# Two-layer decoder trunk on one core: rows of 2 KB for the first down weights of the two-chunk part, the reload of x behind the last streamed block, another order of the last sums, two lows by subtraction

## The chip, the cores and the metric

One core of a Trainium2 chip. The metric is device time in microseconds. The kernel before takes 1773.45 us, the median of three runs (1772.48 to 1774.38). Lower is better.

## The reference, cut to what matters

x is 1024 tokens of 1024 channels in float32. Two layers; in each a token mixer (layer 0 a causal convolution module, layer 1 a multi-scale pooling) and then a dense SwiGLU feed-forward of width 2816, each with RMS norm, shift, scale and gate from a conditioning vector, and a last RMS norm.

```python
def swiglu_ffn(h, w_gate, w_up, w_down):
    return (jax.nn.silu(h @ w_gate) * (h @ w_up)) @ w_down
...
        h = modulate(rms_norm(x, norm_ffn_g[i]), sh_f, sc_f)
        y = swiglu_ffn(h, ffn_w_gate[i], ffn_w_up[i], ffn_w_down[i])
        x = x + (1.0 + g_f)[:, None, :] * y
    return rms_norm(x, final_g)
```

The change touches only the feed-forward of layer 1.

## The kernel before

**Numbers and tiles.** Channels lie on the 128 partitions, tokens run along the free dimension. The tokens are cut into two chunks, A (the first 512) and B. Each float32 operand is split into a high part, `hi`, and the rest, `lo`, both of a rounded type that TensorE takes at full rate. A product is three matmuls, hi by hi, hi by lo and lo by hi, 128x128 weights against 128x512 activations. The width 2816 is 22 tiles `f`.

**Two ways to make a low part of a weight.** A weight arrives as `raw` by a DMA from SyncE's queue (SP) and ScalarE (ACT) copies it to `hi`. Then either VectorE (DVE) subtracts, `lo = raw - hi`, or ACT writes the rounded weight with its sign turned into `lo` and an accumulating DMA on GpSimd's queue (POOL) adds the weight from DRAM to it (`load_weight` with `summed`, L451 to L465, and `low_by_dma`, L1211). Units whose weights are marked `Own` (L608 to L631) take the subtraction.

**The feed-forward of layer 1** runs in three stages, all in the order in which `trunk` writes them at its end (L2164 to L2198):

1. Tiles f = 0 to 7 for chunk A alone (`ffn_p1`, `ffn_p2`).
2. *The two-chunk part*, `ffn_joint` (L1762): tiles f = 8 to 21 for both chunks, as 2x2 blocks with seven products in place of eight. A `joint_unit` (L1621) is one gate or one up matrix of a pair of tiles; it runs the blocks w11, w12, s2, s1, s3, s4 and w22, four steps k of three matmuls each (`block`, L1641). Some block operands don't fit on chip: `t1` and `t4` are kept in DRAM and read back for every unit (`streamed`, L1611, on the SP queue), `t4` for the last block, w22.
3. Tiles f = 0 to 7 for chunk B alone, the first two by `ffn_p1`, the others in pairs (`ffn_mixed`, L1362, with `final(A)`, the last norm of chunk A, beside them).

**The first end of the two-chunk part.** While the first joint unit runs, the down products of f = 6, 7 for chunk A are owed: eight outputs `d` of six matmuls, from four weight tiles of two outputs each (`JointDowns`, L1441, on `Downs`, L1224). Their lows come by an accumulating DMA each (`early`, L1247 to L1250); its source is two slices of `wdn`, so a row of it in DRAM is 1 KB and there are 256 rows. Behind them the block s2 begins. It needs `t2`, whose last piece DVE and ACT make at that time in `joint_rows` (L1564); they also make the last piece of `t4`, which is stored to DRAM and read back.

**The second end.** Within the two-chunk part x of chunk A lies in DRAM (`st["kept", "x"]`): the down products of each pair (`Seven`, L1486) are scaled into a tile `scaled` and added to it by accumulating DMAs on the POOL queue (L1547). In the last unit x comes back by eight DMAs of 256 KB on the POOL queue (L1753 to L1755). Each waits until its tile on chip is free and its row in DRAM is complete. Behind the last unit come the first tile of stage 3 (`before[:1]`, gate and up of f = 0 for chunk B), the down products of f = 20, 21 for both chunks (`last[:1]`, d = 0 to 3), the second tile (f = 1), and `last[1:]`, d = 4 to 7. The order of the sums is `JointDowns.todo`: for each d first A, then B.

PE's order is the order of the code. The orders of ACT, DVE, POOL and SP come out of a scheduler that the build runs. An instruction of a queue waits behind those ahead of it, and a DMA that has to wait holds up its queue.

Of the kernel before, what the change touches and what calls it, by code (L numbers as in the profile page):

```python
# [14 lines left out]
MUL, ADD, SUB = ALU.mult, ALU.add, ALU.subtract  # L15

P = 128
# [4 lines left out]
NF = F // P  # L22
# [37 lines left out]
WHOLE = 8  # L60
# [61 lines left out]


@with_exitstack
def trunk(ctx, tc, xT, c, vec, ada, adan, w1, w2, wgu, wdn, wpl, wph, out):
    nc = tc.nc
    ctx.enter_context(tc.manual_schedule(engines={mybir.EngineType.PE}))
    clock = {"PE": 0.0, "V": 0.0, "G": 0.0, "S": 0.0}
# [5 lines left out]
    last_mm, fixed = [None], [0.0025]  # L134
    synced = mybir.DependencyInfo(mybir.DependencyClass.Sync, mybir.DependencyReason.DATA)
    behind = [False]
# [7 lines left out]
    def order(ins):  # L144

        if behind[0] and last_mm[0] is not None:
            tc.add_manual_dep(ins.ins, last_mm[0], edge, reason="behind the products")
        return ins
# [378 lines left out]
    class Squares:  # L527
# [5 lines left out]
        def add(self, k):  # L533
            ch = self.ch
            if self.acc is None:
                self.acc = bank("acc") if self.psum else temp(ch.n, "acc", 2)
                S_.activation(self.acc, x[ch.i][k], AF.Square)
            else:
                sq = temp(ch.n)
                S_.activation(sq, x[ch.i][k], AF.Square)  # L540
                was = self.acc
                if self.psum and k == KT - 1:
                    self.acc = temp(ch.n, "acc", 2)
                V_.tensor_tensor(self.acc, was, sq, op=ADD)
# [69 lines left out]
    def own(unit_):  # L614
        return unit_[0], tuple(Own(w) for w in unit_[1])
# [608 lines left out]
    class Downs:  # L1224
# [13 lines left out]
        def load(self, dp):  # L1238
            if dp in self.tiles or dp not in self.dps:
                return  # L1240
            self.fetch()
            i = self.dps.index(dp)
            raw = self.raw[:, :, i * 2 * P : (i + 1) * 2 * P]
            wt = wts.tile([P, D], F32R, tag="w", name=nm("w")).rearrange("p (s f d) -> p s f d", s=2, f=2)
            with tc.high_priority(offset=-PREPARED):
                S_.copy(wt[:, 0], raw)
                if getattr(self, "early", False):  # L1247
                    S_.activation(wt[:, 1], raw, AF.Copy, scale=-1.0)
                    src = wdn[self.l, self.fs[0] : self.fs[0] + 2].rearrange("f p d -> p f d")[:, :, dp * 2 * P : (dp + 1) * 2 * P]
                    order(nc.gpsimd.dma_start(wt[:, 1], src, accum_op=ADD))  # L1250
                else:
                    V_.tensor_tensor(wt[:, 1], raw, f32(wt[:, 0]), op=SUB)
            self.tiles[dp] = wt
# [108 lines left out]
    def ffn_mixed(ch, l, plain, until, at_end=False, beside=None):  # L1362

        soon = plain == 2
        before = []
        for f in range(0, plain, 2):
            before += [ffn_p1(ch, l, f, True), ffn_p1(ch, l, f + 1, True, soon)]
            if f:
                before.insert(-1, own(ffn_p2(ch, l, [f - 2, f - 1], True)))
        mates = [Pair(ch, l, f, which) for f in range(plain, until, 2) for which in range(2)]  # L1370
        mine, theirs = [None] * len(mates), []
        for i, f in enumerate(range(plain - 2, until - 2, 2)):
            first, second = Downs(ch, l, (f, f + 1), (0, 1)), Downs(ch, l, (f, f + 1), (2, 3))
            for at, d in ((2 * i + 1, first), (2 * i + 2, second)):
                if at < len(mates):
                    mine[at] = d
                else:
                    theirs.append(d)
        last, = theirs
        before.insert(-1, (lambda take: mine[1].fetch(), ()))  # L1380
        paired = [(lambda take: mates[0].prepare(soon), ())]
        for i, me in enumerate(mates):
            if i + 1 == len(mates):
                paired.append((lambda take: reserve.__setitem__(0, 2), ()))
            paired.append(ffn_pair(ch, l, me, mates[i + 1] if i + 1 < len(mates) else None, mine[i], (mine + [last])[i + 1], soon and i == 0))
            if i == 1 and beside is not None:
                paired.append((lambda take: T.__setitem__(beside[0], Task(beside[1]())), ()))
        paired.append((lambda take: last.load(last.dps[1]), ()))
        if at_end:
            return before, paired, [alone(last), ending(ch, l, [until - 2, until - 1])]  # L1390
        rest = ffn(ch, l, True, at_end, until, ffn_p2(ch, l, [until - 2, until - 1], True))
        rest[1:1] = [alone(last)]
        rest[-3:-1] = rest[-2], rest[-3]
        for i in (4, -1):
            rest[i] = own(rest[i])
        return before, paired, rest
# [44 lines left out]
    class JointDowns(Downs):  # L1441


        def __init__(self, l, fs, dps, chs):
            super().__init__(None, l, fs, dps)
            self.todo = [(d, ch) for d in self.todo for ch in chs]

        def slot(self, out=None):
            d, ch = self.todo.pop(0)
# [171 lines left out]
    def joint_unit(l, me, following, downs, later, first=False, last=False):  # L1621

        def emit(take):
            wt = take()
# [9 lines left out]
            a, left, right = bank(name), bank(name), bank(name)  # L1634
# [3 lines left out]
            slots_at = () if first else SLOTS  # L1638
            at = [0]

            def block(out, part, acts, start):  # L1641
                for k, act in enumerate(acts):
                    cols = slice(k * P, (k + 1) * P)
                    for i, (wp, x_) in enumerate(((0, 0), (0, 1), (1, 0))):
                        matmul(out, w[part][wp][:, cols], act[x_], start=start and k + i == 0, stop=k == half - 1 and i == 2,
                               skip_group_check=True)
                    at[0] += 1
                    if at[0] in slots_at and downs:
                        for each in downs:
                            if each.todo:  # L1650
                                each.slot()
                                break
# [78 lines left out]
            if last:  # L1731
                for k, t in enumerate(front):
                    hi, lo = front[k] = slot(A, "hhi"), slot(A, "hlo")
                    S_.copy(hi, t)
                    V_.tensor_tensor(lo, t, f32(hi), op=SUB)
            block(a, "w22", t4, False)
            if last:
                st["h", 1] = front + hb[half:]
            else:
# [10 lines left out]
            if up and last:  # L1750
                for key, at_ in (("g11", (0, 0)), ("g21", (0, 1)), ("g12", (1, 0)), ("g22", (1, 1))):
                    st["g", at_[0], me.f + at_[1]] = st["blocks"][key]
                x[0] = x_first()  # L1753
                for t, src in zip(x[0], st["kept", "x"]):
                    nc.gpsimd.dma_start(t, src)  # L1755
            elif up:
                V_.scalar_tensor_tensor(qa, qb, -1.0, qa, op0=MUL, op1=SUB)
                given("t4", qa)
# [3 lines left out]
    def ffn_joint(l, start):  # L1762

        mates = [Joint(l, f, which) for f in range(start, NF, 2) for which in range(2)]
        whole = lambda f, chs: [JointDowns(l, (f, f + 1), dps, chs) for dps in ((0, 1), (2, 3))]
        mine = [whole(start - 2, (A,)), []]
        for f in range(start, NF - 2, 2):
            mine += [[Seven(l, (f, f + 1), half)] for half in range(2)]
        mine += [[each] for each in whole(NF - 2, (A, B))]

        mates[0].early = True
        for each in mine[0]:
            each.early = True

        def begin(take):
            mates[0].front()
            for each in mine[0]:
                for dp in each.dps:
                    each.load(dp)
        us = [(begin, ())]  # L1780
        for i, me in enumerate(mates):
            later = mine[i + 1]
            us.append(joint_unit(l, me, mates[i + 1] if i + 1 < len(mates) else None, mine[i], later[0] if later else None,
                                 i == 0, i + 1 == len(mates)))
        (second,), (final,) = mine[-2:]
        return us, [alone(second, final), alone(final)]
# [64 lines left out]
    def final(ch):  # L1851
        acc = yield from sum_sq(x[ch.i], ch.n, wide("acc"))
        rstd = yield from mean_rsqrt(acc, ch.n, True)
        for k in range(KT):
            xs = x[ch.i][k]
            V_.scalar_tensor_tensor(xs, xs, V("final_g", k), rstd, op0=MUL, op1=MUL)
            nc.sync.dma_start(out[:, k, ch.t0 : ch.t0 + ch.n], xs)
            yield
# [66 lines left out]
    for k in range(KT + 1):  # L1925
# [13 lines left out]
        if k < KT:  # L1939
# [6 lines left out]
            t = temp(A.n)  # L1946
# [243 lines left out]
    joint, last = ffn_joint(1, WHOLE)  # L2190
    add(joint)
    before, pairs, rest = ffn_mixed(B, 1, 2, WHOLE, True, ("final_a", lambda: final(A)))
    add(before[:1])
    put_eager(("T", 1), lambda: combined(B, (A, A, B, B)))

    add(last[:1] + before[1:] + last[1:])
    paired(B, pairs)
    add(rest)  # L2198
# [54 lines left out]
```

## Time and profile before

The profiled execution took 1771.89 us; its span, first to last instruction, is 1770.1 us.

| | busy us | share of the span |
|---|---|---|
| PE (matmul) | 1738.5 | 98% |
| DVE | 1374.0 | 78% |
| ACT | 987.1 | 56% |
| POOL | 564.0 | 32% |
| DMA, mean of 16 engines | | 207 GB/s over the span |

Times below count from the start of the span. The chain that ended last is 89% PE, so an idle stretch of PE is time of the kernel. The two-chunk part runs from about 1180 to 1602 us. A row of the timeline gives start, duration, engine, line, what is written and read, how often, and in brackets the idle time before it with what ended it. A row of windows gives the stretch, its length, PE's busy time with its matmuls, the granted clock (1.00 is full), the DMA engines' share and the rate.

### The profile page before, as it was taken

The page shows a single profiled execution, that of the slowest core. Times are in us where ns is not written, and L with a number is a line of the kernel's source. Part 1 is how long each engine was busy: PE and PEld are TensorE (multiplying, and loading weights), DVE is VectorE, ACT ScalarE, POOL GpSimd, SP SyncE. Part 2 cuts the span into 40 slices and gives each one's busy share as a digit, 9 for nine tenths or more (in the row PEclk, how much of TensorE's full clock was granted, in tenths as well). Part 3 has the DMA queues.
Part 4 walks back from the last instruction along what each step waited for, and adds up shares of the span by engine and source line. Part 5 has one row for each costly group of instructions (what it writes and reads, how often), then busy time and mean ns, then how long its engine had stood idle before and what let it go on. Part 6 is the DMA issues. An engine that isn't in the chain of part 4 may idle for free.

```text
span 1770.1 us, 24916 instructions
## 1 busy us (share of the span) xinstructions
PE 1738.5 (98%) x8830; PEld 1460.3 (82%) x8830; DVE 1374.0 (78%) x2273; ACT 987.1 (56%) x1566; POOL 564.0 (32%) x607
## 2 busy tenths in 40 slices
PE   9999999999999999999999999999999999999997
PEld 7777787788888888899999888887888888877996
DVE  7999657788775327989996977976888788777885
ACT  4776656767656455555555356464444444444653
POOL 0599614887834121211102713411011111111112
PEclk9999999999999999999999999999999999999999
DMA  9959746988988988877675477798778888887551
GB/s 296 305 171 251 196 118 157 243 214 213 240 204 205 240 218 195 222 210 215 198 213 132 123 179 177 166 235 272 226 216 262 240 242 223 252 251 201 155 150 54
DMA packets 145151, 366.26 MB, mean 207 GB/s; under 512 B 14977, under 2 KB 32641, under 8 KB 145026
## 3 DMA queue, kind: packets, MB, share of 16 engines
q1 hardware_dynamic: 109600, 265.56, 44.5%
q0 software_dynamic: 34272, 98.06, 31.3%
q8 instruction: 69, 1.13, 0.3%
q10 hardware_dynamic: 1154, 1.05, 0.2%
q14 instruction: 56, 0.46, 0.1%
HBM read 340.50 MB, written 24.12 MB: 206 GB/s over the span
## 4 chain that ended last, share of the span: by engine, by line
PE 89%; DMA 4%; issue 2%; DVE 2%; ACT 1%; POOL 1%; SPq 0%; DVEq 0%; POOLq 0%; ACTq 0%
PE gate L142 24%; PE dn L142 24%; PE up L142 23%; PE y L142 6%; PE a L142 3%; PE g L142 3%; PE first L142 2%; DMA adaw<-in_adan_dram 1%; DMA t<-t 1%; DMA w<-in_wdn_dram 1%; PE ada L142 1%; DMA front<-front 1%; DVE x L119 1%; ACT w L119 0%; DMA w<-in_wgu_dram 0%
## 5 line engine op out<-in xcount | busy, mean ns | idle before, releaser
L119 ACT CAST w<-raw 128x1024 fp32r<-128x1024 f32 (+1 forms) x314 | 262.7, 838 | 110.6 <-PE up L142 46.1
L142 PE MATMUL dn<-ghi,w 128*128 128x512 f32 (+1 forms) x944 | 302.6, 386 | 2.7 <-DMA w<-in_wdn_dram 2.1
L142 PE MATMUL gate<-hhi,w 128*128 128x512 f32 (+1 forms) x968 | 295.1, 373 | 1.3 <-ACT hhi L119 0.8
L142 PE MATMUL up<-hhi,w 128*128 128x512 f32 (+1 forms) x968 | 294.6, 372 | 0.0
L119 ACT ACTIVATE w<-raw 128x1024 fp32r<-128x1024 f32 (+1 forms) x182 | 172.9, 950 | 193.1 <-PE up L142 60.0
L119 DVE SCALAR_TENSOR_TENSOR x<-dn,gains,x 128x512 f32<-128x512 f32 (+1 forms) x312 | 225.5, 733 | 46.9 <-PE dn L142 45.2
L142 PEld LDWEIGHTS gate<-hhi,w 128*128 128x128 f32 x968 | 178.1, 189 | 34.6 <-ACT hhi L119 1.0
L142 PEld LDWEIGHTS dn<-ghi,w 128*128 128x128 f32 x944 | 176.3, 189 | 36.6 <-DMA w<-in_wdn_dram 2.5
L142 PEld LDWEIGHTS up<-hhi,w 128*128 128x128 f32 x968 | 178.0, 188 | 31.8
L142 PE MATMUL dn<-glo,w 128*128 128x512 f32 (+1 forms) x472 | 181.9, 385 | 0.1
L142 PE MATMUL gate<-hlo,w 128*128 128x512 f32 (+1 forms) x484 | 180.2, 372 | 0.3 <-DVE hlo L119 0.3
L142 PE MATMUL up<-hlo,w 128*128 128x512 f32 (+1 forms) x484 | 179.8, 372 | 0.0
L119 DVE SCALAR_TENSOR_TENSOR ca<-u,taps,ca 128x512 f32<-128x512 f32 x251 | 174.9, 747 | 0.9
L461 POOL DMA_DIRECT2D w<-in_wgu_dram x76 | 69.0, 907 | 247.3 <-ACT w L119 233.2
L1547 POOL DMA_DIRECT2D x<-scaled x48 | 41.6, 868 | 325.9 <-ACT scaled L119 170.2
L119 DVE TENSOR_TENSOR w<-raw,w 128x512 fp32r<-128x512 f32 (+1 forms) x132 | 108.9, 831 | 41.8 <-ACT w L119 34.9
L119 POOL TENSOR_TENSOR pa<-pa,pr 128x512 f32<-128x512 f32 x92 | 131.5, 1509 | 8.4 <-ACT pr L119 6.4
L119 DVE TENSOR_TENSOR t<-t,up 128x512 f32<-128x512 f32 (+1 forms) x76 | 49.4, 650 | 89.7 <-PE up L142 87.1
L1215 POOL DMA_DIRECT2D w<-in_wgu_dram x42 | 37.1, 891 | 256.3 <-ACT w L119 109.5
L119 POOL TENSOR_TENSOR pa<-pa,ny 128x512 f32<-128x512 f32 x77 | 104.0, 1381 | 8.5 <-ACT ny L119 5.8
L142 PEld LDWEIGHTS gate<-hlo,w 128*128 128x128 f32 x484 | 91.3, 189 | 16.6 <-DVE hlo L119 0.6
L142 PEld LDWEIGHTS up<-hlo,w 128*128 128x128 f32 x484 | 91.1, 188 | 15.9
(292 smaller groups left out, 3844.4 us busy)
## 6 DMA issues: line engine op xcount, KB each, us to landing
raw<-in_wgu_dram SPq DMA_DIRECT2D x148, 512.0 KB, 5.6
t<-t SPq DMA_DIRECT2D x224, 256.0 KB, 5.2
w<-in_wgu_dram POOLq DMA_DIRECT2D x76, 512.0 KB, 8.2
adaw<-in_ada_dram SPq DMA_DIRECT2D x64, 512.0 KB, 5.1
raw<-in_wdn_dram SPq DMA_DIRECT2D x62, 512.0 KB, 5.5
raw<-in_w_dram SPq DMA_DIRECT2D x42, 512.0 KB, 6.2
w<-in_wdn_dram POOLq DMA_DIRECT2D x34, 512.0 KB, 8.3
adaw<-in_adan_dram SPq DMA_DIRECT2D x32, 512.0 KB, 5.7
```

The lines of the kernel that those rows point to most:

```text
L119: self.last = self.order(getattr(self.eng, name)(out, *args, **kw))
L142: last_mm[0] = nc.tensor.matmul(out, lhsT, rhs, start=start, stop=stop, **kw).ins.name
L461: order(nc.gpsimd.dma_start(as_src(lo), src, accum_op=ADD))
L1215: order(nc.gpsimd.dma_start(lo, src, accum_op=ADD))
L1547: order(nc.gpsimd.dma_start(st["kept", "x"][at], t, accum_op=ADD))
```

## The change

Four edits. (1) The sources of the four early low DMAs come from a new DRAM array `wdp`, made on the host, in which the 512 numbers that a partition takes lie side by side: 128 rows of 2 KB for 256 of 1 KB. The hi parts and raw loads stay. (2) The eight reloads of x wait, by a semaphore, for the matmul that stood last on PE when step k = 3 of the last block w22 was written: the end of its step k = 2. (3) The last down sums run chunk by chunk, B first and then A. (4) Gate and up of f = 0 for chunk B (`before[0]`) are `Own`: DVE subtracts the two lows, in place of an ACT pass and an accumulating DMA of 512 KB each.

```diff
@@ Downs.load
                 if getattr(self, "early", False):
                     S_.activation(wt[:, 1], raw, AF.Copy, scale=-1.0)
-                    src = wdn[self.l, self.fs[0] : self.fs[0] + 2].rearrange("f p d -> p f d")[:, :, dp * 2 * P : (dp + 1) * 2 * P]
-                    order(nc.gpsimd.dma_start(wt[:, 1], src, accum_op=ADD))
+                    order(nc.gpsimd.dma_start(wt[:, 1].rearrange("p f d -> p (f d)"), wdp[dp], accum_op=ADD))
@@ JointDowns.__init__
-            self.todo = [(d, ch) for d in self.todo for ch in chs]
+            self.todo = [(d, ch) for ch in chs for d in self.todo]
@@ joint_unit
-            def block(out, part, acts, start):
+            def block(out, part, acts, start, came=None):
                 for k, act in enumerate(acts):
                     cols = slice(k * P, (k + 1) * P)
+                    if came is not None:
+                        came.append(last_mm[0])
...
-            block(a, "w22", t4, False)
+            came = []
+            block(a, "w22", t4, False, came)
...
                 for t, src in zip(x[0], st["kept", "x"]):
-                    nc.gpsimd.dma_start(t, src)
+                    d = nc.gpsimd.dma_start(t, src)
+                    tc.add_manual_dep(d.ins, came[3], synced, reason="behind the streamed block")
@@ ffn_joint
-        mine += [[each] for each in whole(NF - 2, (A, B))]
+        mine += [[each] for each in whole(NF - 2, (B, A))]
@@ trunk
     before, pairs, rest = ffn_mixed(B, 1, 2, WHOLE, True, ("final_a", lambda: final(A)))
+    before[0] = own(before[0])
     add(before[:1])
@@ kernel
+        "wdp": A(np.asarray(ffn_w_down)[1, (WHOLE - 2) * P : WHOLE * P].reshape(2, P, 4, 2 * P).transpose(2, 1, 0, 3).reshape(4, P, 4 * P)),
```

The POOL queue at the second end, before. `x_22..<-scaled` are the accumulations into x in DRAM, `x_0_28..<-x_22..` the reloads, `w_..<-in_wgu` the lows of weights: `w_2785` and `w_2788` those of gate and up of f = 0, `w_2833` and `w_2841` those of f = 1.

```order
L461 DMA w_2785_14761<-in_wgu_dram 128x1024
L1547 DMA x_2270_11672<-scaled_2297_11793 128x512
L1547 DMA x_2271_11673<-scaled_2297_11793 128x512
L1755 DMA x_0_2823_15001<-x_2268_11670 128x512
L1755 DMA x_0_2824_15002<-x_2269_11671 128x512
L1755 DMA x_0_2825_15003<-x_2270_11672 128x512
L461 DMA w_2788_14768<-in_wgu_dram 128x1024
L1755 DMA x_0_2826_15004<-x_2271_11673 128x512
L1755 DMA x_0_2827_15005<-x_2272_11674 128x512
L1755 DMA x_0_2828_15006<-x_2273_11675 128x512
L1547 DMA x_2274_11676<-scaled_2297_11793 128x512
L461 DMA w_2833_15020<-in_wgu_dram 128x1024
```

The same place after the change (line numbers of the changed kernel):

```order
L1546 DMA x_2271_11673<-scaled_2297_11793 128x512
L1757 DMA x_0_2823_14999<-x_2268_11670 128x512
L1757 DMA x_0_2824_15000<-x_2269_11671 128x512
L1757 DMA x_0_2825_15001<-x_2270_11672 128x512
L1757 DMA x_0_2826_15002<-x_2271_11673 128x512
L1757 DMA x_0_2827_15003<-x_2272_11674 128x512
L1757 DMA x_0_2828_15004<-x_2273_11675 128x512
L1546 DMA x_2274_11676<-scaled_2297_11793 128x512
L461 DMA w_2833_15018<-in_wgu_dram 128x1024
L1546 DMA x_2275_11677<-scaled_2297_11793 128x512
L461 DMA w_2841_15082<-in_wgu_dram 128x1024
L1757 DMA x_0_2829_15005<-x_2274_11676 128x512
```

The two lows of f = 0 are gone, the first six reloads stand together, the first of them with the new wait, and the lows of f = 1 stand behind them; the low of up of f = 1 now also stands ahead of the last two reloads.

DVE in the last joint unit after the change, around the first subtraction that is added (`scaled<-dn` and `x<-dn` read PSUM banks into which PE adds the next product; `hlo` is a low of chunk B's activations, `t<-t,up` the unit's own sums):

```order
L119 TENSOR_TENSOR hlo_14962<-front_14827,hhi_14961 128x512
L119 TENSOR_TENSOR w_14761<-raw_14758,w_14760 128x1024
L119 TENSOR_TENSOR t_14773<-t_14773,up_14771 128x512
L119 SCALAR_TENSOR_TENSOR scaled_11793<-dn_14815,gains,scaled_11793 128x512
L119 TENSOR_TENSOR hlo_14966<-front_14829,hhi_14965 128x512
L119 TENSOR_TENSOR t_14773<-t_14773,sg_14750 128x512
L119 SCALAR_TENSOR_TENSOR scaled_11793<-dn_14839,gains,scaled_11793 128x512
L119 TENSOR_TENSOR ring_11796<-acc_14729,ring_11796 128x256
L119 TENSOR_TENSOR hlo_14970<-front_14831,hhi_14969 128x512
L119 TENSOR_TENSOR hf_15086<-hhi_14957,hlo_14958 128x512
L119 SCALAR_TENSOR_TENSOR x_2_87<-dn_14790,gains,x_2_87 128x512
L119 SCALAR_TENSOR_TENSOR x_3_88<-dn_14802,gains,x_3_88 128x512
```

Before, the subtraction of `w_14761` is not there; the reads of `dn` stand in the same order among themselves, while three rows that PE doesn't wait for here (`t<-t,sg`, `hf` and a low of `gpair`) have moved by a few places. The second added subtraction, of `w_14767`, stands four rows behind the last row shown. At the first end the orders of ACT, DVE, POOL and SP are as before.

More of the change, by code (lines that the diff above doesn't have):

```diff
@@ L124, in trunk @@
 @with_exitstack
-def trunk(ctx, tc, xT, c, vec, ada, adan, w1, w2, wgu, wdn, wpl, wph, out):
+def trunk(ctx, tc, xT, c, vec, ada, adan, w1, w2, wgu, wdn, wdp, wpl, wph, out):
     nc = tc.nc
```

## The prediction

> **What bounds the kernel now.** I first read the page's busy times, then the view of waits for PE.
>
> ```profile
> PE 1738.5 (98%) x8830; PEld 1460.3 (82%) x8830; DVE 1374.0 (78%) x2273; ACT 987.1 (56%) x1566; POOL 564.0 (32%) x607
> ...
> PE dn L142 <- DMA w<-in_wdn_dram: 5.8, 3, 3.1
> ...
> PE up L142 <- DMA t<-t: 3.1, 2, 2.5
> ```
>
> PE is the bound, so only PE's idle or slow time can be won. The two waits stand at the two ends of the two-chunk part, where the edits are. A row of the windows shows what the second costs, the idle time and the clock together:
>
> ```profile
> 1578.94:1602.21 23.27, 18.92 (x77) 0.94 0.95 274
> ```
>
> PE is busy for 18.9 of 23.3 us, the granted clock is 0.94, and the DMA engines are 95% taken. The matmul's own pace is in a row of the chain of waits:
>
> ```profile
> 1256.79 1.36 PE gate L142 x6
> ```
>
> Six in 1.36 us: 0.227 us each at full clock. This is the price of every matmul below.
>
> *First end*, PE's timeline:
>
> ```profile
> 1201.77 6.05 PE L142 MATMUL dn<-gpair,w 128*128 128x512 f32 x26
> 1208.36 3.02 PE L142 MATMUL dn<-gpair,w 128*128 128x512 f32 x12 [0.54 <-DMA w<-in_wdn_dram]
> 1214.51 4.64 PE L142 MATMUL dn<-gpair,w 128*128 128x512 f32 x10 [3.13 <-DMA w<-in_wdn_dram]
> ...
> 1222.48 0.39 PE L142 MATMUL gate<-t1hi,w 128*128 128x512 f32 x1
> ...
> 1233.61 0.73 PE L142 MATMUL gate<-t,w 128*128 128x512 f32 x2 [0.17 <-DMA t<-t]
> ```
>
> The third and fourth weight tile's lows come late (26 matmuls in, then 38 in). Behind the 3.13 us, ten matmuls take 4.64 us, half clock. The 48 `dn` and the 12 of s2 need 60 x 0.227 = 13.6 us, so t1 could begin at 1215.4; it begins at 1222.5. **7.1 us** are lost here at most.
>
> *Second end*, PE's timeline again:
>
> ```profile
> 1595.46 0.84 PE L142 MATMUL up<-t,w 128*128 128x512 f32 x3
> 1596.86 0.50 PE L142 MATMUL up<-t,w 128*128 128x512 f32 x1 [0.56 <-DMA t<-t]
> 1599.91 1.22 PE L142 MATMUL up<-t,w 128*128 128x512 f32 x2 [2.55 <-DMA t<-t]
> ...
> 1602.21 0.63 PE L142 MATMUL gate<-hhi,w 128*128 128x512 f32 x1
> ```
>
> From 1595.46 nine matmuls are left before `gate`: 9 x 0.227 = 2.0 us, so `gate` could begin at 1597.5 and begins at 1602.2. **4.7 us** are lost, waiting for the last pieces of the streamed t4.
>
> **Edit 1, rows of 2 KB.** Why are the lows late? POOL's timeline, ACT's, and the landings:
>
> ```profile
> 1186.30 0.88 POOL L1215 DMA_DIRECT2D w<-in_wgu_dram  x1 [9.43 <-ACT w L119]
> 1187.38 1.24 POOL L1250 DMA_DIRECT2D w<-in_wdn_dram  x1 [0.20 <-issue]
> 1195.09 1.22 POOL L1250 DMA_DIRECT2D w<-in_wdn_dram  x1 [6.47 <-ACT t L119]
> 1201.24 1.20 POOL L1250 DMA_DIRECT2D w<-in_wdn_dram  x1 [4.93 <-ACT t2hi L119]
> 1208.66 1.22 POOL L1250 DMA_DIRECT2D w<-in_wdn_dram  x1 [6.22 <-ACT w L119]
> ...
> DMA to landing us min/median/max: 5.8/6.4/7.4
> ...
> 1192.14 0.63 ACT L119 ACTIVATE w<-raw 128x512 fp32r<-128x512 f32 x1
> ```
>
> ACT is done with the last of the four at 1192.8, so the ACT names in brackets are not the reason. The four are issued 7.7, 6.2 and 7.4 us apart, as far as each takes to land: only one of this form is in flight. The form with 2 KB rows, elsewhere in the program, does better:
>
> ```profile
> 744.69 1.82 POOL L1215 DMA_DIRECT2D w<-in_wgu_dram  x2 [0.40 <-issue]
> 746.85 0.86 POOL L1215 DMA_DIRECT2D w<-in_wgu_dram  x1 [0.34 <-ACT w L119]
> 752.86 0.88 POOL L1215 DMA_DIRECT2D w<-in_wgu_dram  x1 [5.14 <-issue]
> ...
> DMA to landing us min/median/max: 7.9/7.9/7.9
> ```
>
> Three are issued within 3 us and the fourth at 752.86, just behind the landing of the first (744.69 + 7.9 = 752.6). So the queue holds so many rows, and half the rows let three in. Then here: the w12 low at 1186.3 and the first two `wdp` at once; the third when the w12 low has landed, about 1191; the fourth when the first `wdp` has, 1187.4 + 7.9 = 1195. With the longest landing of these forms, 7.9, it is there at 1203. PE wants it 38 matmuls behind 1201.8, at 1210.4. Both waits go, with 7 us to spare.
>
> What is late next is DVE, not PE:
>
> ```profile
> 1216.63 0.75 DVE L119 SCALAR_TENSOR_TENSOR x<-dn,gains,x 128x512 f32<-128x512 f32 x1 [4.02 <-PE dn L142]
> ...
> 1219.19 0.75 DVE L119 SCALAR_TENSOR_TENSOR x<-dn,gains,x 128x512 f32<-128x512 f32 x1 [1.21 <-PE dn L142]
> ...
> 1221.06 0.69 DVE L119 TENSOR_TENSOR t2lo<-t,t2hi 128x512 fp32r<-128x512 f32 x1
> ...
> 1222.26 0.69 DVE L119 TENSOR_TENSOR t<-whole,t 128x512 fp32r<-128x512 f32 x1
> ```
>
> The row at 1216.63 says that DVE had work up to 1212.6, when PE could have been through with `dn`. It waits for PE only then, 4.02 + 1.21 = 5.2 us. Only these 5.2 us can go, so t2lo is done at 1221.75 - 5.2 = 1216.5, while PE, through with `dn` at 1212.7, wants it ten matmuls later, at 1214.9: a new wait of 1.6 us. And t4's last piece (DVE at 1222.26, then stored and read back; the bracket at 1233.61 shows its last read already ends PE's wait before) also moves by 5.2: PE reaches it about 1 us too early. The end of the unit thus moves with DVE: **-5.2 us**, of at most 7.1; below, 3.5, if the low DMAs, now earlier among the stores and raw loads of 1187 to 1200, hold up DVE's inputs by 2 us. I take 5.2, since DVE's rows have no gap there that a DMA ends.
>
> The Trainium skill speaks against this edit: "DMA: Bandwidth & Descriptors", section Specifications, gives 512 B as the least transfer at line rate, so rows of 1 KB are long enough and longer ones bring nothing. By it the edit is worth 0 and the sum below only 4.7. For one transfer the rows agree, 5.8 to 7.4 us with 1 KB, 7.9 with 2 KB; how many are in flight the page's figure doesn't say.
>
> **Edits 2 and 4, the second end.** The last t4 piece lands late:
>
> ```profile
> 1585.70 14.16 DMA t<-t
> ...
> q0 software_dynamic: 226, 0.68, 76.4%
> q1 hardware_dynamic: 212, 0.40, 24.7%
> ```
>
> The two lower rows are the DMA view of 1584.0 to 1588.9: POOL's queue takes 76% of the engines' time, SP's with t4 25%. What POOL moves there:
>
> ```profile
> 1579.91 0.87 POOL L461 DMA_DIRECT2D w<-in_wgu_dram  x1 [9.73 <-ACT w L119]
> ...
> 1584.11 0.86 POOL L1755 DMA_DIRECT2D x<-x  x1
> ...
> 1593.21 1.65 POOL L1755 DMA_DIRECT2D x<-x  x3 [0.56 <-PE up L142]
> ```
>
> Edit 4 takes away the first (and a second of 512 KB), edit 2 the reloads; the two accumulates of 256 KB that stand between them in the order stay. From the rows above, SP's queue needs 24.7% of 4.9 us for 0.40 MB, 3.0 us for one MB, and POOL's 5.5. Left from 1580 on: 2 MB of t4 and 0.5 MB of a raw weight, 7.5 us, and 0.5 MB of accumulates, 2.8 us: all landed by about 1592, and PE wants t4's last piece at 1596. The waits and the half clock behind them go: **-4.7 us**; at least 2, if the accumulates and t4's own eight loads make half of the lateness.
>
> *What edit 2 adds.* POOL now waits until about 1596 and then issues six reloads. Behind them stand the lows of f = 1, whose first PE wants after gate and up of f = 0 (24 matmuls each) and the sums (48), 1597.5 + 96 x 0.227 = 1619.3. At 1593.2 three reloads go out in 1.65 us, so six are out by 1600 and, with 7.9 us as at 744.7, down by 1608; the low follows when the first two are down, at about 1605, and lands by 1613 with the median of its like:
>
> ```profile
> w<-in_wgu_dram POOLq DMA_DIRECT2D x76, 512.0 KB, 8.2
> ```
>
> Hidden, by 6 us. Edit 3 puts B's four sums (5.4 us) ahead of A's, whose reloads are thus wanted at 1613.8 for the first: nothing is late, and the edit alone costs and gains 0, in the same count of matmuls.
>
> *What edit 4 adds*: two subtractions on DVE.
>
> ```profile
> L119 DVE TENSOR_TENSOR w<-raw,w 128x1024 fp32r<-128x1024 f32 x10 | 14.5, 1450 | 0.0
> ...
> 1584.55 1.40 DVE L119 SCALAR_TENSOR_TENSOR x<-dn,gains,x 128x512 f32<-128x512 f32 x2
> ...
> 1586.62 0.84 PE L142 MATMUL dn<-t,ring 128*128 128x512 f32 x3
> ...
> 1601.17 0.69 DVE L119 SCALAR_TENSOR_TENSOR t<-up,ny 128x512 f32<-128x512 f32 x1 [4.39 <-PE up L142]
> ```
>
> 1.45 us each. The first moves the read of the bank `x<-dn`, 0.75 long, from 1584.55 to at most 1586.0, done at 1586.75; PE writes that bank again at 1586.62: 0.1 us at most, and less since one row of 0.6 us moved behind it. Before 1601.17 DVE idles 4.39 us, which takes in both. Price 0, at most 0.3. ACT loses two passes and isn't waited for by more.
>
> **The sum.** Profiled execution 1771.89 - 5.2 - 4.7 = 1762.0. The median shown is 1.56 above that execution, so the forecast is **1763.5**. The bounds: -7.1 - 4.7 gives 1761.6 for the median, -3.5 - 2 + 0.3 gives 1768.2; the three runs spread by 1 us to each side.
>
> **Rivals.**
> 1. *t4 stays late* by its own eight loads and the accumulates: half of the second term, 1773.45 - 5.2 - 2.3 = 1766.0. For it: DMA engines 95% taken over the whole window. Against: POOL's 76%. Chance 0.13.
> 2. *Longer rows bring nothing* (the rule above): still one at a time, first end as before, 1768.7. Against: the three at 744.7. Chance 0.11.
> 3. *The gains return as other waits*: DVE, or the next unit's streams, take the first gain back at 1222 to 1245, and half of the second fails: 1773.45 - 2.3 = 1771.1, no change. Chance 0.07.
> 4. *Slower*: the reloads block POOL. If they went one at a time, 7.9 us each, the first low of f = 1 would go out at 1596 + 6 x 7.9 = 1643 and land 8.2 later, 32 us too late: 1773.45 - 9.9 + 32 = 1796. It decides where fewer than three are in flight: two make 1596 + 24 + 8.2 = 1628, 9 us too late and nothing gained. Against: the three in 1.65 us. Chance 0.06.
>
> The forecast has 0.63 (its own range 1761.5 to 1765.2). The range must take in rivals 1 and 2: 1760.5 to 1769.0, leaving 0.13 out. About 0.2% (3.5 us) is what a measurement can tell from no change. Faster 0.87, same 0.07, slower 0.06.
>
> **What would show it.** Right: the four `wdp` DMAs issued by 1196, no PE wait for `w<-in_wdp`, a new short wait of PE for DVE's t2lo near 1215 and for `t<-t` at the unit's end; at the second end no wait for `t<-t`, clock 1.00, six reloads in one burst near PE's last block. Wrong: `wdp` issues 6 us apart; t4's last landing over 10 us; PE waiting for `w<-in_wgu` at gate or up of f = 1; DVE ending PE's waits in the last unit.

## The result, and the profile after

The changed kernel takes **1762.33 us**, the median of six runs (1760.50 to 1765.75), beside 1772.97 us (1770.69 to 1774.38) for the kernel before in the same series: a ratio of 0.9942, 95% interval 0.9929 to 0.9954, or 8.2 to 12.6 us less. The profiled execution took 1760.5 us.

The windows of before, cut at the two ends (stretch, length, PE's busy time with its matmuls, granted clock, DMA share, GB/s):

```profile
0.00:1201.77 1201.77, 1190.26 (x6132) 1.00 0.78 206
1201.77:1234.18 32.41, 28.57 (x110) 0.89 0.79 249
1234.18:1578.26 344.08, 344.08 (x1519) 1.00 0.83 242
1578.26:1602.21 23.95, 19.60 (x80) 0.94 0.93 269
1602.21:1770.10 167.89, 156.01 (x995) 0.98 0.50 129
```

The same windows of after, cut at the same matmuls:

```profile
0.00:1200.24 1200.24, 1189.34 (x6132) 1.00 0.78 206
1200.24:1228.28 28.04, 26.18 (x110) 1.00 0.82 286
1228.28:1572.47 344.19, 344.19 (x1519) 1.00 0.82 242
1572.47:1591.46 18.99, 17.99 (x80) 1.00 0.63 197
1591.46:1758.70 167.24, 155.63 (x995) 0.98 0.51 139
```

The second row is the *first stretch*: from the first early down product to the first `up` product of that unit. The fourth is the *second stretch*: from the first of the last ten down groups to the first `gate` of f = 0. Of the 11.40 us between the two spans, 4.37 went in the first stretch and 4.96 in the second, and the clock of both is 1.00 now. The last row gives 0.65 more, of which 0.39 lie in the 48 products of gate and up of f = 0 (11.27 us before, 10.88 after): before, they began at half clock. The first row's 1.53 us lie ahead of every edit; over the profiles below the first stretch begins anywhere from 1200.2 to 1204.9. So kernels are compared by the two stretches and by medians, not by one span.

*First end after.* PE's timeline, then POOL's, DVE's and SP's:

```profile
1200.24 11.04 PE L142 MATMUL dn<-gpair,w 128*128 128x512 f32 x48
1214.86 0.50 PE L142 MATMUL gate<-t2lo,w 128*128 128x512 f32 x1 [1.31 <-DVE t2lo L119]
...
1224.98 1.18 PE L142 MATMUL gate<-t,w 128*128 128x512 f32 x3 [0.17 <-DMA t<-t]
```

```profile
1184.78 0.88 POOL L1215 DMA_DIRECT2D w<-in_wgu_dram  x1 [9.42 <-ACT w L119]
1185.82 0.87 POOL L1249 DMA_DIRECT2D w<-in_wdp_dram  x1 [0.16 <-issue]
1187.38 0.87 POOL L1249 DMA_DIRECT2D w<-in_wdp_dram  x1 [0.69 <-ACT w L119]
1188.84 0.89 POOL L1249 DMA_DIRECT2D w<-in_wdp_dram  x1 [0.59 <-ACT t3hi L119]
1193.21 0.88 POOL L1249 DMA_DIRECT2D w<-in_wdp_dram  x1 [3.48 <-ACT t L119]
...
DMA to landing us min/median/max: 7.0/7.4/7.8
```

```profile
1214.10 0.70 DVE L119 TENSOR_TENSOR t2lo<-t,t2hi 128x512 fp32r<-128x512 f32 x1
...
1215.30 0.71 DVE L119 TENSOR_TENSOR t<-whole,t 128x512 fp32r<-128x512 f32 x1
```

```profile
1215.43 2.32 SPq L1504 DMA_DIRECT2D raw<-in_wdn_dram  x2
1217.85 4.59 SPq L152 DMA_DIRECT2D t<-t  x9
```

All 48 down products run without a gap; the four lows, one at a time before, go out within 8 us. PE then waits 1.31 us for DVE's t2lo and three times 0.2 us for t4's last pieces. DVE is done with t4's last low at 1216.01, but two raw loads stand ahead of its store on SP, and the store goes out at 1217.85.

*Second end after*, PE's timeline and POOL's:

```profile
1590.78 0.84 PE L142 MATMUL dn<-t,ring 128*128 128x512 f32 x3
1591.46 0.39 PE L142 MATMUL gate<-hhi,w 128*128 128x512 f32 x1
```

```profile
1590.63 3.31 POOL L1757 DMA_DIRECT2D x<-x  x6 [11.88 <-PE up L142]
1594.02 0.90 POOL L1546 DMA_DIRECT2D x<-scaled  x1
1596.83 0.90 POOL L461 DMA_DIRECT2D w<-in_wgu_dram  x1 [1.91 <-issue]
...
DMA to landing us min/median/max: 3.1/5.0/7.0
```

No wait for `t<-t` is left there. The six reloads go out in one burst (the last row is theirs), and the low of f = 1 follows at 1596.83.

### The profile page after: what moved, and what is told of

The parts are those of the page before. It is cut to its first block, busy times and chain, and to the rows that moved or that the text cites. A ratio compares the mean times of both kernels' runs of the same rounds, so it can differ in the third digit from the quotient of the medians.

```text
span 1758.7 us, 24908 instructions
## 1 busy us (share of the span) xinstructions
PE 1733.3 (99%) x8830; PEld 1456.9 (83%) x8830; DVE 1374.2 (78%) x2275; ACT 987.7 (56%) x1564; POOL 561.7 (32%) x605
## 4 chain that ended last, share of the span: by engine, by line
PE 92%; DVE 3%; DMA 2%; POOL 1%; ACT 1%; issue 1%; SPq 0%; DVEq 0%; POOLq 0%; ACTq 0%
PE dn L142 25%; PE gate L142 25%; PE up L142 24%; PE y L142 6%; PE a L142 3%; PE g L142 3%; PE first L142 2%; PE ada L142 1%; DVE x L119 1%; POOL pa L119 1%; DMA front<-front 1%; PE var L142 1%; PE rstd L142 1%; DMA w<-in_wdn_dram 1%; DMA w<-in_wgu_dram 0%
```

## The experiments

All are made on the changed kernel unless said. The expectations describe the second stretch loosely: their "last three groups" with 21.0 us are eleven, their "last six" ten; 18.99, 23.95 and 24.96 are in the measure of the windows above. Stretches are from one profile each, times are medians (n runs) with the ratio to before and its interval.

| kernel | first, us | second, us | time, us | ratio |
|---|---|---|---|---|
| before | 32.41 | 23.95 | 1772.97 (6) | |
| before_again | 32.26 | 24.96 | 1776.85 (1) | |
| after | 28.04 | 18.99 | 1762.33 (6) | 0.9942 [0.9929, 0.9954] |
| rows_1kb | 29.70 | 19.48 | 1764.36 (5) | 0.9953 [0.9941, 0.9966] |
| x_unbound | 27.49 | 18.55 | 1761.28 (5) | 0.9936 [0.9922, 0.9949] |
| lows_by_dma | 26.74 | 20.50 | 1762.10 (5) | 0.9945 [0.9933, 0.9957] |
| sums_mixed | 26.74 | 18.96 | 1761.92 (5) | 0.9941 [0.9929, 0.9954] |
| array_1kb | 31.05 | 18.76 | 1765.42 (1) | |
| two_1kb | 27.15 | 18.78 | 1763.84 (1) | |
| both_ahead | 25.62 | 18.97 | 1762.26 (5) | 0.9940 [0.9926, 0.9954] |
| end_undone | 26.88 | 24.28 | 1767.93 (11) | 0.9968 [0.9955, 0.9981] |
| ahead_unbound | 26.42 | 18.64 | 1760.52 (5) | 0.9924 [0.9907, 0.9941] |
| store_first | 26.71 | 19.00 | 1761.90 (1) | |
| lows_cut4 | 27.75 | 19.04 | 1764.18 (5) | 0.9955 [0.9937, 0.9972] |

### Each edit undone

**rows_1kb**, edit 1 undone:

```diff
-                    order(nc.gpsimd.dma_start(wt[:, 1].rearrange("p f d -> p (f d)"), wdp[dp], accum_op=ADD))
+                    src = wdn[self.l, self.fs[0] : self.fs[0] + 2].rearrange("f p d -> p f d")[:, :, dp * 2 * P : (dp + 1) * 2 * P]
+                    order(nc.gpsimd.dma_start(wt[:, 1], src, accum_op=ADD))
```

> The changed kernel with edit 1 undone: the four early down lows come again from the weight itself, in 256 rows of 1 KB each; edits 2, 3 and 4 stay. Theory (rows in flight): POOL issues them one at a time again, 6 to 8 us apart, PE waits about 0.5 and 3 us for them at half clock afterwards, and the stretch of PE from the first early down product to the first `up` product of that unit lasts 32.4 us as before instead of 28.0. The stretch at the second end (first of the last three groups of down products to the first `gate` product of f = 0) stays at 21.0. Time about 4.4 us over the changed kernel: 1766.7, a ratio to before of 0.9965. Rival (longer rows bring nothing, the first end gained otherwise): the stretch stays near 28 and the time at 1762.3, 0.994.

The lows went out at 1187.6, 1194.6, 1200.4 and 1206.7, one at a time. PE's timeline shows one wait:

```profile
1202.00 8.77 PE L142 MATMUL dn<-gpair,w 128*128 128x512 f32 x38
1212.96 3.76 PE L142 MATMUL dn<-gpair,w 128*128 128x512 f32 x10 [2.19 <-DMA w<-in_wdn_dram]
```

The stretch is 29.70, with clock 0.94: the loss is back, though not the whole 32.4. The lows landed in 5.5 to 6.6 us here, in 5.8 to 7.4 in the first profile of before; over four in a row that is 1.8 us, and PE waits once. The rival's 28 is missed. The median lies 2 us above after's, not the 4.4 expected, and the intervals of the two ratios overlap.

**before_again**, the kernel before once more:

> The kernel before, unchanged, profiled a second time: how far its first profile is typical of the two ends. First profile: PE's stretch from the first early down product to the first `up` product of that unit 32.4 us, with waits of 0.54 and 3.13 us for the third and fourth low; the stretch from the first product of the last six down groups to the first `gate` product of f = 0 24.0 us (18.99 in the changed kernel). Theory A (typical): 31.5 to 33 and 23 to 25 again. Theory B (the first end was unusually long in that profile, as rows_1kb with its 29.7 us and a single wait of 2.2 us suggests): the first stretch at 29.5 to 30.5.

The waits are 0.64 and 3.29 us for the lows, the stretches 32.26 and 24.96: the first profile was typical, and rows_1kb's end was a short one.

**x_unbound**, edit 2 undone:

```diff
-                    d = nc.gpsimd.dma_start(t, src)
-                    tc.add_manual_dep(d.ins, came[3], synced, reason="behind the streamed block")
+                    nc.gpsimd.dma_start(t, src)
```

> The changed kernel with edit 2 undone: the reloads of x wait for no product of PE; edits 1, 3 and 4 stay. Theory A (what counts is the bytes ahead of t4's last pieces, and edits 2 and 4 share the work): the reloads go out from about 1578 beside t4's loads; t4's last piece lands some 4 us later than the 1586.4 of the changed kernel, about when PE wants it (1590); PE waits 0 to 1.5 us, the second stretch lasts 21.0 to 23, the time is up by 0 to 2 us (1762.3 to 1764.3). Theory B (edit 2 alone frees t4): PE's waits for t<-t of 0.6 and 2.5 us are back, the stretch lasts 26, the time is up by 5 us to 1767.3. The first stretch stays at 28.0 in both.

PE doesn't wait for `t<-t` at the second end, though the reloads go out beside t4's loads from 1579.2 and t4's last piece lands at 1589.3. The stretch is no longer than after's. Edit 2 alone is worth nothing while edit 4 stands.

**lows_by_dma**, edit 4 undone:

```diff
-    before[0] = own(before[0])
```

> The changed kernel with edit 4 undone: the two lows of 512 KB of the first unit after the joint part are made by accumulating DMAs on POOL's queue again, without the two subtractions on DVE; edits 1, 2 and 3 stay. Theory A (bytes ahead of t4, shared between edits 2 and 4): at most one such DMA is in flight beside t4, t4's last piece lands 2 to 3 us later than 1586.4 and still ahead of PE's 1590: no wait of PE for t<-t, second stretch 21.0 to 21.5, time 1762.3 within 0.7. Rival (the low, an accumulate, holds up t4 more than the plain reloads do): PE waits 2 us or more for t<-t, second stretch 23.5 or more, time up by 2.5 us or more.

```profile
PE up L142 <- DMA t<-t: 0.9, 3, 0.4
```

Three short waits at the second end, 0.9 us in all, and t4's last piece lands at 1591.8, 12.2 us behind its issue: between the theory and the rival. The stretch is 1.5 us longer; the median shows nothing.

**end_undone**, both undone:

> The changed kernel with edits 2 and 4 both undone: the reloads of x wait for no product, and the two lows of 512 KB come by accumulating DMAs; edits 1 and 3 stay. Alone, edit 2 undone cost the second stretch -0.4 us (18.55 against 18.99) and edit 4 undone +1.5 (20.50). Theory (either part alone still leaves POOL's queue room beside t4's loads, both together don't): PE's waits for t<-t of 2.5 to 4 us in all are back, second stretch 23.5 to 25 us as in the two profiles of the kernel before (23.95, 24.96), half clock after the waits, time 5 to 6 us above the changed kernel: 1767 to 1768.5. Rival (the costs add): second stretch 20 to 20.7, time within 1.5 us of 1762.3. The first stretch stays at 26.7 to 28 in both.

```profile
PE up L142 <- DMA t<-t: 3.5, 2, 2.3
```

The costs don't add: -0.4 and +1.5 alone, **+5.3 together** (24.28 against 18.99), and 5.6 us in the median (4.6 by the ratios). The delays of t4 nearly do. Counted from the start of the stretch, its last piece lands at 13.9 us in after (13.4 to 14.9 in the seven profiles with both edits), 15.6 in x_unbound, 19.2 in lows_by_dma and 22.0 here: against after, 1.7 and 5.3 us later for one edit undone and 8.1 for both. PE comes to the product that reads this piece at 17.9 in after, so the first 3 to 4 us of delay cost nothing; that is why x_unbound is free and why the costs don't add. Either edit alone takes most of the second term. Since edits 1 and 3 are all that is left here, its ratio of 0.9968 is theirs: 3.4 to 8.0 us.

**sums_mixed**, edit 3 undone:

```diff
-            self.todo = [(d, ch) for ch in chs for d in self.todo]
+            self.todo = [(d, ch) for d in self.todo for ch in chs]
...
-        mine += [[each] for each in whole(NF - 2, (B, A))]
+        mine += [[each] for each in whole(NF - 2, (A, B))]
```

> The changed kernel with edit 3 undone: the sums of the last two groups go row by row, each for A and then for B, instead of B's four first; edits 1, 2 and 4 stay. Theory: costs and gains 0, since the first six reloads have landed by 1600.4 and A's first sum is done at about 1603.7: no new wait of PE, both stretches as in the changed kernel (28.0, 21.0), time 1762.3 within 0.7. Rival (edit 2 needs edit 3: A's last reloads, which land at 1612 to 1614, are late for the sums that now come first): DVE waits for a reload, a bank of the sums stays taken, PE waits for DVE in the 48 products behind 1602 or has a clock below 1.00 there, time up by 1 us or more.

No new wait, the second stretch 18.96, the time as after's. Edit 3 is worth nothing.

### What holds the early lows: rows, not their length

**array_1kb** lays `wdp` out by halves, so that a DMA has 256 rows of 1 KB, the rows of a half one behind the other in memory:

```diff
-                    order(nc.gpsimd.dma_start(wt[:, 1].rearrange("p f d -> p (f d)"), wdp[dp], accum_op=ADD))
+                    order(nc.gpsimd.dma_start(wt[:, 1], wdp[dp].rearrange("f p d -> p f d"), accum_op=ADD))
...
-.reshape(2, P, 4, 2 * P).transpose(2, 1, 0, 3).reshape(4, P, 4 * P))
+.reshape(2, P, 4, 2 * P).transpose(2, 0, 1, 3))
```

> The changed kernel, but the extra array of down weights is laid out so that each low comes in 256 rows of 1 KB instead of 128 of 2 KB; the rows of one half lie one behind the other in memory, where the kernel before took 1 KB pieces out of rows of 4 KB. Theory (room in POOL's queue goes by rows): one of these DMAs is in flight at a time, issues 5.5 to 7.5 us apart, the fourth lands at about 1213, PE waits 2 to 3 us for it, first stretch 29.5 to 32.4. Rival (the scattered source was slow, not the number of rows): three go out within 4 us as with 2 KB rows (1185.8, 1187.4, 1188.8), no wait of PE, first stretch 26.7 to 28.

POOL's timeline of array_1kb, with the landings of the four:

```profile
1187.82 1.24 POOL L1249 DMA_DIRECT2D w<-in_wdp_dram  x1 [0.20 <-issue]
1194.58 1.22 POOL L1249 DMA_DIRECT2D w<-in_wdp_dram  x1 [5.53 <-ACT w L119]
1201.84 1.20 POOL L1249 DMA_DIRECT2D w<-in_wdp_dram  x1 [6.04 <-issue]
1209.57 1.22 POOL L1249 DMA_DIRECT2D w<-in_wdp_dram  x1 [6.53 <-issue]
...
DMA to landing us min/median/max: 5.5/6.7/7.4
```

**two_1kb** takes the same array by two DMAs of 128 rows:

```diff
-                    order(nc.gpsimd.dma_start(wt[:, 1], wdp[dp].rearrange("f p d -> p f d"), accum_op=ADD))
+                    for f in range(2):
+                        order(nc.gpsimd.dma_start(wt[:, 1, f], wdp[dp, f], accum_op=ADD))
```

> The same array as in array_1kb, but each low is fetched by two DMAs of 128 rows of 1 KB, so eight DMAs of half the bytes in place of four. Theory (room goes by rows, whatever their length): three of them in flight at a time, as with rows of 2 KB, the next always about 0.3 us behind a landing; each lands 4 to 7 us after its issue, so the eighth goes out by 1201 and lands by 1207, ahead of PE's 1209: no wait, first stretch 26.7 to 28. Rival 1 (room goes by bytes): five or six of them out at once behind the low of w12, the eighth issued by 1195. Rival 2 (rows of 1 KB are served one DMA at a time whatever else): issues 3 to 6 us apart, the eighth at 1210 or later, PE waits over 2 us, stretch over 29.

POOL's timeline of two_1kb:

```profile
1190.06 1.76 POOL L1250 DMA_DIRECT2D w<-in_wdp_dram  x2 [0.16 <-issue]
1193.05 0.89 POOL L1250 DMA_DIRECT2D w<-in_wdp_dram  x1 [1.22 <-ACT t3hi L119]
1197.34 1.85 POOL L1250 DMA_DIRECT2D w<-in_wdp_dram  x2 [3.41 <-issue]
1200.31 0.87 POOL L1250 DMA_DIRECT2D w<-in_wdp_dram  x1 [1.11 <-issue]
1204.16 0.89 POOL L1250 DMA_DIRECT2D w<-in_wdp_dram  x1 [2.99 <-issue]
```

With 256 rows each the new array helps nothing: issues 6.8, 7.3 and 7.7 us apart, one in flight, PE waits of 1.0 and 2.8 us, 31.05. With 128 rows of the same 1 KB, three are in flight and PE waits for none of them, 27.15; three at a time although each moves half the bytes. So an accumulating DMA takes room in POOL's queue by its rows. The eighth went out at 1205.5; this profile's first stretch begins 4.2 us later than after's, so that is the 1201 expected. It landed at 1211.9, about 1 us ahead of PE.

This settles the rule that the prediction weighed. The Trainium skill, "DMA: Bandwidth & Descriptors", section Specifications, has 512 B as the least transfer at line rate, so that rows of 1 KB are long enough. By row length the runs agree with it: 27.15 with 1 KB rows, 26.7 to 28.0 with 2 KB. What the edit gains comes from half the rows in a DMA, which that figure doesn't touch.

### What holds the first end now

**both_ahead** puts the lows of the first unit's s2 and s1 weights behind t4's last low on DVE, and the next unit's raw loads behind t4's last store on SP; **store_first** does only the second:

```diff
             V_.tensor_tensor(tiles[1], q, f32(tiles[0]), op=SUB)
+            st["low"] = V_.last.ins.name
...
-                sync.dma_start(dst, f32(t))
+                st["stored"] = sync.dma_start(dst, f32(t))
...
+            if k == half - 1:
+                st["t4 low"] = st["low"]
...
+            def behind_t4():
+                if "t4 low" in st:
+                    tc.add_manual_dep(V_.last.ins, st["t4 low"], edge, reason="behind the stored block")
...
                 self.halves("s2", s2)
+                behind_t4()
                 self.halves("s1", s1)
+                behind_t4()
...
-                nc.sync.dma_start(t, wdn[self.l, self.fs[f], :, h * QUAD + first : h * QUAD + first + H])
+                d = nc.sync.dma_start(t, wdn[self.l, self.fs[f], :, h * QUAD + first : h * QUAD + first + H])
+                if "stored" in st:
+                    tc.add_manual_dep(d.ins, st["stored"].ins.name, edge, reason="behind the stored block")
...
```

> The changed kernel with two orders altered at the first end, nothing else: on DVE the lows of the first unit's later weights (s2, s1) wait behind t4's last low, so that t2lo and t4's last low come some six rows earlier; on SP the raw loads of the next unit's down weights wait behind the store of t4's last piece. Theory (DVE's order and SP's order hold the first end now): t2lo is done before PE has finished the 48 down products, PE's wait of 1.3 us for t2lo goes, t4's last piece is read back by about 1222, the waits of 0.2 us for t<-t go; first stretch 25.0 to 25.8 instead of 26.7 to 28.0, time 1 to 2.5 us below the changed kernel's 1762.3. Rival (the late update rows of x keep the banks of the down products taken, or s2's low is late): PE gets a new wait for DVE inside the 48 products or at s2, and the stretch stays at 26.7 or longer.

PE's timeline of both_ahead:

```profile
1204.93 11.04 PE L142 MATMUL dn<-gpair,w 128*128 128x512 f32 x48
...
1228.63 1.15 PE L142 MATMUL gate<-t,w 128*128 128x512 f32 x3 [0.19 <-DMA t<-t]
1229.97 0.73 PE L142 MATMUL gate<-t,w 128*128 128x512 f32 x2 [0.19 <-DMA t<-t]
```

DVE has t2lo done at 1211.8, PE wants it behind 1215.8: the wait is gone and the stretch is 25.62, as the theory has it, near the 25.0 that 110 matmuls take at 0.227. t4's pieces still end two waits of 0.2 us. The median doesn't show the 1.1 to 2.4 us.

> The changed kernel with one order altered on SP: the four raw loads of the next unit's down weights stand behind t4's last store and its eight reloads, where two of them stood ahead of that store. DVE's order is the changed kernel's. Theory A (DVE holds the first end, SP's order costs a little): PE's wait of 1.3 us for t2lo stays, t4's last store goes out within 0.3 us of DVE's last low instead of 0.7 to 1.8, PE's waits for t<-t go, first stretch 26.3 to 26.7 (25.6 with DVE's order altered). Theory B (SP's order alone holds it): stretch under 26. Theory C (the raw loads were wanted where they stood): a new wait of PE for ACT or DVE in the next unit's ring products, time up by 1 us or more.

26.71, with the wait of 1.3 us for t2lo: theory A, but for one wait of 0.2 us for t4 that stays. Without SP's condition lows_by_dma and sums_mixed have 26.74, so DVE's order holds this end, SP's little, and the gain of both_ahead is DVE's in the main. There t4's last store goes out at 1213.76, right behind DVE's last low, and the next unit's raw loads only at 1224.45; how much of that the condition on SP did isn't shown, since no run has DVE's order altered alone.

**ahead_unbound** joins both_ahead and x_unbound:

> The best of what has been seen: the order of DVE as in both_ahead (the lows of the first unit's later weights behind t4's last low) and edit 2 undone (reloads of x unbound), on top of edits 1, 3 and 4. Theory (the two ends are independent): first stretch 25.6, second 18.5, 1.9 us less than the changed kernel's usual 27.2 and 18.9 together; time 1759.5 to 1761.5. Rival (the gain at the first end comes back in the stretch between the ends or behind them): the two stretches as said, the time at 1762 or more.

1760.52 us, the lowest median, with a first stretch of 26.42 (25.6 expected; three waits of 0.2 us for t4) and a second of 18.64. It is below before by 0.6 to 0.9%. That it beats the changed kernel, 1.8 us away with overlapping intervals, isn't shown.

### Why t4 was late

**lows_cut4** is end_undone with each of the two lows of 512 KB in four DMAs of 128 rows of 1 KB:

```diff
-            order(nc.gpsimd.dma_start(as_src(lo), src, accum_op=ADD))
+            for i in range(cut):
+                part = slice(i * n // cut, (i + 1) * n // cut)
+                order(nc.gpsimd.dma_start(*((as_src(lo), src) if cut == 1 else (lo[:, part], src[:, part])), accum_op=ADD))
```

> The kernel end_undone (edits 2 and 4 undone) with one thing altered: each of the two lows of 512 KB comes by four accumulating DMAs of 128 rows of 1 KB instead of one of 128 rows of 4 KB, the same bytes in the same queue. In end_undone POOL's queue took 78.8% of the DMA engines' time and SP's, with t4, 27.4% over the 5 us in which t4's last pieces wait (0.73 and 0.45 MB). Theory (a DMA engine takes turns between the two queues, so many rows at a time, and POOL's rows are the longer ones): with short rows POOL's share there falls to 40 to 60%, SP's rises to 45 to 60%, t4's last piece lands within 10 us of its issue instead of 14.7, PE's waits for t<-t fall from 3.5 us to under 1, second stretch 19 to 21, unless a low of f = 0, now in four pieces of which three are in flight, comes late and PE waits for w<-in_wgu instead. Rival (bytes alone decide): POOL's share stays over 70%, t4's last piece takes 13 us or more, PE waits 3 us or more, stretch 24 as in end_undone.

The DMA view of end_undone, 1580 to 1585 (packets, MB, share of the engines), with t4's landings:

```profile
q0 software_dynamic: 264, 0.73, 78.8%
q1 hardware_dynamic: 241, 0.45, 27.4%
...
DMA to landing us min/median/max: 4.5/10.9/14.7
```

The same place in lows_cut4, 1582 to 1587:

```profile
q1 hardware_dynamic: 698, 1.27, 69.1%
q0 software_dynamic: 356, 0.32, 40.5%
...
DMA to landing us min/median/max: 4.2/6.2/6.8
```

The same bytes stand in POOL's queue, and t4 is in time: no wait for `t<-t`, 19.04. The median is 3.8 us below end_undone's, with overlapping intervals of the ratios. So the bytes that stand in the queue don't decide alone. But fewer of them were on their way: room goes by rows, and when t4's last load went out, three pieces with 384 KB were in flight, where end_undone had 1280 KB. The accumulations of x went out behind t4's loads in lows_cut4, and among them in end_undone. Either this or the shorter rows in each turn brought t4 forward; this run doesn't part the two.

The Trainium skill, "DMA: Bandwidth & Descriptors", section Queues, rings and completion order, says that an engine takes the queues in turn, a packet of descriptors at a time. If a turn held as many rows of either queue, the queue with the longer rows would get more. In end_undone that fits: 264 and 241 packets of the view (a packet is about one row) are nearly one to one, while the bytes stand 0.73 to 0.45. Elsewhere it doesn't: 356 to 698 in lows_cut4, and 256 to 525 in x_unbound from 1580 to 1585, are one to two. So even turns of rows aren't shown. In x_unbound, where only 256 KB transfers are in POOL's queue, t4's last piece took 9.2 us.

## Why the prediction was right, point by point

**The forecast**, 1763.5 us, lies 1.2 above the median. From the profiled execution it expected -9.9; without the 1.53 us ahead of the edits it is -9.86. Both terms are off by under 1 us, in opposite directions; that the sum fits this closely is luck.

**Edit 1, -5.2.** The mechanism held: one accumulating DMA at a time with 256 rows, three with 128, the fourth issued at 1193.2 (1195 expected), landed at 1201.0 (1203), no wait for it; DVE is what is late next, and PE's wait for t2lo is 1.3 us (1.6 expected). The prediction took 7.9 us for the longest landing; that is the first of the three at 744.7, and the other two took 9.5 and 10.5. Here the longest is 7.8, and 10.5 would have been in time too. The term itself measured 4.4 in after's profile, where t4's last store went out 1.84 us behind DVE's last low, after 2.32 us of SP for two raw loads. In the six other profiles with edit 1 and DVE's order unchanged (x_unbound, lows_by_dma, sums_mixed, end_undone, store_first, lows_cut4) the stretch is 26.7 to 27.75, or 4.5 to 5.7 below the two profiles of before. So 5.2 was right in size, and after's own profile is at the long end. The bound of 7.1 is near: both_ahead is 6.6 to 6.8 below before.

**Edits 2 and 4, -4.7.** Measured are 4.96 and the 0.39 of the slow matmuls behind `gate`, which the term left out, as it did 0.24 us of a shorter wait for `scaled`. The mechanism held: transfers on POOL's queue made t4 late. Its last piece was forecast for about 1592 (the two terms, 7.5 and 2.8 us from 1580 on, add up to 1590.3) and landed at 1586.4 in a stretch that begins 5.8 us earlier, so at 1592.2 in the time of before. The price of 5.5 us for one MB fits the two lows, 5.3 us for the MB that lands ahead of t4 in lows_by_dma. It is too high for plain reloads: in x_unbound two of them, 0.5 MB, land ahead of t4's last piece, and it comes 1.7 us later. The 4 us between this 1592 and PE's 1596 are slack, and the prediction didn't draw from them that one edit would nearly do: plain reloads beside t4 cost nothing, the two lows of 512 KB cost 1.5 us, and the whole loss needs both. The floor of 2 us stood for half of the lateness staying; as the runs show, either edit alone would have kept 3.8 us or more.

**What edit 2 adds.** Hidden, as said, and earlier than said: all six reloads go out in 3.31 us, the first landing 3.1 us behind its issue where 7.9 was taken, so the low of f = 1 leaves at 1596.8 and not 1605. PE begins f = 1 at 1613.2, with no wait.

**Edit 3, 0**, shown by sums_mixed. **Edit 4's subtractions, 0 to 0.3**: no wait of PE for DVE at the second end.

**The rivals.** *t4 stays late* exists in small, 0.9 us, in lows_by_dma, but not with both edits. *Longer rows bring nothing* is true of the length and false of the edit. *The gains return*: the stretch between the ends is 344.08 and 344.19 us. *Slower*, reloads blocking POOL: more than the three that it needed are in flight.

## What to carry to other kernels

A queue that issues DMAs only as earlier ones land is seen in the intervals between issues being as long as the landings, whatever the engine named as releaser; there, count rows per DMA before bytes. Two edits at one place cost 0 and 1.5 us when undone alone and 5 together, because the first 3 to 4 us of delay were slack; so undo both as well, and compare when the late transfer lands and not only how long PE waits. Gains of 1 to 2 us in 1760 were not visible in medians of five runs; they were in the waits within stretches cut at the same matmuls, though such a stretch itself differs by 1.3 us between kernels that are alike there.

## What the runs showed of the hardware

- POOL's queue holds three accumulating DMAs of 128 rows, whether of 1 or 2 KB. Of 256 rows of 1 KB it holds one (array_1kb, rows_1kb), with one of 128 rows beside it (in before, issued at 1208.66 and 1209.38, the first landing at 1214.5). The next goes out about 0.3 us behind a landing (1188.84 behind 1188.53 in after). Of plain reloads of 128 rows of 2 KB six were in flight (six issues from 1590.63 to 1593.4, the first landing 3.1 us behind the first issue). Six copies fit and four accumulations don't, so a copy takes less than two thirds of the room of an accumulation.
- The granted clock fell in a stretch with a single wait of 2.19 us (0.94 in rows_1kb) and not with one of 1.31 us (1.00 in the first stretch of after) or of 1.50 us (1.00 in the second stretch of rows_1kb).
- The first stretch differs by 1.3 us between profiles of kernels that are alike there: 26.7 in lows_by_dma and sums_mixed, 28.0 in after. One issue among some ten on SP takes 1.1 to 1.9 us there in place of 0.3 to 0.4, at changing places; in after it was a raw load ahead of t4's store.
